# Transposed products of a decoder trunk: each tile's low matmul placed directly behind its high one

## Chip, core and metric

The kernel runs on one core of a Trainium2 chip. The metric is the device time of one execution in microseconds (us), as the median of several runs; beside it stands one execution taken by the hardware profiler, with a record of every instruction. TensorE is PE in the profile (PEld its weight loads), VectorE DVE, ScalarE ACT, GpSimd POOL, and SP the queue that issues most DMAs.

## What is computed

A decoder trunk of two layers on 256 tokens of width 2048 in float32: layer 0 mixes with a gated DeltaNet, layer 1 with sparse attention under an indexer; each layer goes on with a layer norm, a gated MLP of width 5120, another layer norm and a gated addition. Cut to its outline:

```python
for i in range(DEPTH):                                   # DEPTH = 2
    h = gdn_mixer(x, ...) if i % 2 == 0 else dsa_mixer(x, ...)
    x = layer_norm(DN_ALPHA * x + h, ln1_g[i], ln1_b[i])
    f = (silu(causal_dwconv(x @ ffn_w_gate[i], ffn_conv_w[i])) * (x @ ffn_w_up[i])) @ ffn_w_down[i]
    x = layer_norm(DN_ALPHA * x + f, ln2_g[i], ln2_b[i])
    x = x + sigmoid(x @ ple_w_gate[i]) * (p[i] @ ple_w_proj[i])
```

Nearly all of the work is products of x, or of what was made from it, with weight matrices that are read once.

## The kernel before

**High and low parts.** Each float32 operand of a weight product is held as two float32r numbers, a high part and what is left of it, the low part. A product is high x high + low x high + high x low. For x both parts lie in xT, [128, 16 row tiles, 2 parts, 256 tokens]. For a weight, `weights` (L86) loads a block of 512 KB into `raw` (4 buffers), ACT copies it to `hi` (L96), and DVE subtracts that from `raw` to give `lo` (L97). `hi` and `lo` have two buffers each: the `hi` of a block is written into the buffer of the block two earlier, as soon as PE has done its last matmul with it. `high_priority` lets the scheduler place both far ahead.

**Two kinds of products.** `gemm_steps` (L125) gives [tokens, columns]; the change leaves it alone. `gemm_t_steps` (L100) gives the transpose, [columns, tokens], and takes 256 columns of weights as two tiles of 128, each with a PSUM bank `q` of its own. One block is 4 row tiles of those 256 columns; 4 blocks make a sum. For each row tile and each column tile there are two matmuls: one with `hi` as the stationary operand, over both parts of x (512 columns, into the whole of q, L113), and one with `lo` over the high part of x alone (256 columns, into the second half of q, L117). So a block has 8 of the first and 8 of the second. Their order in a block is written out by the two loops at L111 and L115. There are 4176 of each in the program, in the DeltaNet's keys, queries and values, the indexer and the attention, and the MLP's gate and up projections.

**What follows a sum.** When the fourth block is done, the caller's `done` folds the halves of q: ACT copies the second half (L166), DVE adds it to the first (L167), and the caller goes on with ACT and DVE (for the MLP's gate a convolution, L621, L623, L625; for its up projection L630 and the split L170, L171).

**Order.** The scheduler of the framework sets one fixed order for each engine; each engine then works strictly in it and waits on semaphores. Between the matmuls of a block it also puts other PE work: in the DeltaNet small products and transposes, at the start of an MLP the layer norm's transposes (L250).

Of the kernel before, what the change touches and what calls it, by code (L numbers as in the profile page):

```python
# [18 lines left out]
D = 2048  # L19
# [10 lines left out]
# Columns of the table of constants.  # L30
# [4 lines left out]
def constants():  # L35
    """Masks, the identity and the buckets of relative distance: functions of the shapes alone."""
    c = np.zeros((P, N_CONST), np.float32)
    i, j = np.arange(P)[:, None], np.arange(P)[None, :]
    c[:, C_IDENT:C_IDENT + P] = i == j
    c[:, C_TRI:C_TRI + P] = i <= j  # L40
    c[:, C_OFF:C_OFF + P] = i // 32 > j // 32
    c[:, C_CMIN:C_CMIN + P] = np.where(j <= i, np.float32(3.4e38), np.float32(-BIG))
    x = np.zeros((4, 32, 8, 32), np.float32)
    for cg in range(4):
        for k in range(8):
            x[cg, :, k, 4 * k + cg] = 1.0
    c[:, C_XINIT:C_XINIT + 256] = x.reshape(P, 256)
    c[:, C_ONES:C_ONES + P] = 1.0
    c[:, C_CAUSAL:C_CAUSAL + P] = j <= i
    d = np.maximum(255 - np.arange(NR), 0)  # L50
    f = np.maximum(d, 1).astype(np.float32)
    large = 16 + (np.log(f / np.float32(16)) / np.float32(math.log(8.0)) * np.float32(16)).astype(np.int32)
    b = np.where(d < 16, d, np.minimum(large, 31))
    return c, (np.arange(32)[:, None] == b[None, :]).astype(np.float32)


def bcast(ap, n, axis):
    """ap with a new axis of n repeats."""
    dims = [list(x) for x in ap.ap]
    dims.insert(axis, [0, n])  # L60
    return bass.AP(tensor=ap.tensor, offset=ap.offset, ap=dims)


class Trunk:
# [21 lines left out]
    def weights(self, src, rows, nk, cols):  # L86
        """src: DRAM [K, N]; the block of nk row tiles from `rows` and `cols` as (hi, lo) [128, nk, ncols]."""
        nc = self.nc
        c0, n = cols
        shape = [P, nk, n]  # L90
        raw = self.wp.tile(shape, F32, tag="raw", name="raw", bufs=4)
        nc.sync.dma_start(out=raw, in_=src[rows:rows + nk * P, c0:c0 + n].rearrange("(k p) n -> p k n", p=P))
        hi = self.wp.tile(shape, F32R, tag="hi", name="hi", bufs=2)
        lo = self.wp.tile(shape, F32R, tag="lo", name="lo", bufs=2)
        with self.tc.high_priority(offset=W_AHEAD):
            nc.scalar.activation(hi, raw, AF.Copy)  # L96
            nc.vector.tensor_tensor(lo, raw, hi.bitcast(F32), op=ALU.subtract)  # L97
        return hi, lo

    def gemm_t_steps(self, src, c0, n, x, done, kt=KT):  # L100
        """Products with the output transposed, [columns, tokens], one call of done(column, psum) per 128
        columns; the sum of the two halves of psum is the product. Yields after each block of weights."""
        nc = self.nc
        for c in range(c0, c0 + n, 256):
            w = min(256, c0 + n - c)
            nt = [(o, min(P, w - o)) for o in range(0, w, P)]
            ps = [self.mm.tile([P, 512], F32, tag="mm", name="mm_ps") for _ in nt]
            nk = 1024 // w
            for k0 in range(0, kt, nk):
                hi, lo = self.weights(src, k0 * P, nk, (c, w))  # L110
                for k in range(nk):  # L111
                    for (o, m), q in zip(nt, ps):
                        nc.tensor.matmul(q[:m, :], hi[:, k, o:o + m], x[:, k0 + k].rearrange("p a b -> p (a b)"),  # L113
                                         start=k0 + k == 0, stop=False)
                for k in range(nk):  # L115
                    for (o, m), q in zip(nt, ps):
                        nc.tensor.matmul(q[:m, S:], lo[:, k, o:o + m], x[:, k0 + k, 0, :],  # L117
                                         start=False, stop=k0 + k == kt - 1)
                if k0 + nk < kt:
                    yield  # L120
            for (o, m), q in zip(nt, ps):
                done((c - c0 + o) // P, q[:m, :])
            yield

    def gemm_steps(self, src, c0, n, x, kt, done):  # L125
        """One block of at most 512 columns, [tokens, columns]: done(half, psum) for each half of the tokens."""
# [21 lines left out]
    @staticmethod  # L148
    def go_(*steps):
        """Runs the products of several calls side by side."""  # L150
        steps = list(steps)
        while steps:
            steps = [g for g in steps if next(g, steps) is not steps]
# [7 lines left out]
    def fold(self, pool, out, ps):  # L161
        """out = the product that gemm_t left in the two halves of ps."""
        nc = self.nc
        m = ps.shape[0]
        t = pool.tile([P, S], F32, tag="fold", name="fold", bufs=2)
        nc.scalar.activation(t[:m], ps[:, S:], AF.Copy)  # L166
        nc.vector.tensor_tensor(out, ps[:, :S], t[:m], op=ALU.add)  # L167
# [5 lines left out]
    def to_xT(self, xT, x, a, k0):  # L173
        """Four row tiles of xT for half a of the tokens from x [128, 512]."""
# [5 lines left out]
    def rows(self, pool, src, n, tag, bufs=1):  # L180
        """A DRAM row of n, in all partitions."""
# [4 lines left out]
    def columns(self, pool, srcs, tag):  # L186
        """DRAM arrays [n, 128], as columns of one tile [128, sum of n]."""
# [13 lines left out]
    def residual(self, xb, ps, st):  # L201
        """x <- ALPHA x + ps for a block of columns, and its moments."""
        self.nc.vector.scalar_tensor_tensor(xb, xb, ALPHA, ps, op0=ALU.mult, op1=ALU.add)
        self.nc.vector.bn_stats(st, xb)

    def moments(self, pool, st, eps):
        """Mean and 1/sqrt(variance + eps) from the statistics st [128, n, 6]."""
# [6 lines left out]
    def rsqrt(self, pool, z, n):  # L214
        """1 / sqrt(z) of z [128, n] > 0, which is overwritten: three Newton steps from a first value within 4%,
        by the exponent."""
# [13 lines left out]
    def layer_norm(self, pool, st, g, b, gb):  # L230
        """x and xT from the sums in x: g and b are rows in DRAM, gb the same as columns."""
# [35 lines left out]
    def gdn_gates(self, pool, w, gk):  # L267
# [7 lines left out]
        # softplus(x) = max(x, 0) + log1p(e), e = exp(-|x|); log1p(e) = 2 atanh(s), s = e / (2 + e) <= 1/3  # L275
# [16 lines left out]
        # beta = 1 / (1 + exp(-b))  # L292
# [4 lines left out]
        # running sums of g within each half of the tokens: as columns, and as rows by way of DRAM  # L297
# [13 lines left out]
    def gdn(self):  # L311
# [3 lines left out]
        with tc.tile_pool(name="gk", bufs=1) as gk, tc.tile_pool(name="gw", bufs=1) as pool:  # L315
            cw = gk.tile([P, 4, 64], F32, tag="cw", name="cw")
            ng = gk.tile([P, 1], F32, tag="ng", name="ng")
            # staged where the groups' tiles will be
# [24 lines left out]
    def gdn_groups(self, pool, gk, cw, ng, oT, load, gates):  # L343
        """Groups of two heads of queries and keys, four of values. In each half of the tokens, with k and q not
        normalised, c = beta / |k|^2: (I + L) u = beta v / |k|, L[t, s] = c_t (k_t . k_s) D[t, s] for s < t;
        o_t = (sum over s <= t of (q_t . k_s) D[t, s] u_s) / |q|. The blocks of 32 on the diagonal of I + L are
        inverted by substitution into T, then I + L = T^-1 (I + W), W = T (L outside the blocks), W^4 = 0."""
# [12 lines left out]
        def conv(n0, out):  # L360
            """gemm_t's consumer: causal convolution of the column tile, then 2 silu() into out(n)."""
# [13 lines left out]
        def decays(s):  # L375
            """D for s <= t, with s in the partitions (within a half: qd; from half to half: qo), and with t (L)."""
# [32 lines left out]
        def sums(s):  # L409
            """Sums of squares of q and k, as columns, and what follows from them."""  # L410
# [24 lines left out]
        def blocks(s):  # L435
# [15 lines left out]
            # the 32 by 32 blocks on the diagonal, one in each partition  # L451
# [12 lines left out]
            # their inverses by columns: column 4 c + e is number c in partition (e, block)  # L464
# [20 lines left out]
        def inverses(s):  # L485
            """T, transposed, and W, transposed."""
# [47 lines left out]
        def outputs(s):  # L534
            """o, normalised and gated, transposed."""
# [111 lines left out]
    def prepare(self, i, pool):  # L647
        """The taps of the MLP's convolution, as columns. The products p Wp: two blocks of columns with each call of
        what is returned, into self.pw."""
# [45 lines left out]
    def distances(self, pool):  # L695
        """The bias by distance in DRAM, F[h, 255 - distance], one copy per query. Yields between its transfers."""
# [19 lines left out]
    def dsa(self, pool, xT, oT):  # L716
# [3 lines left out]
        # indexer keys and head weights  # L720
# [17 lines left out]
        # scores of the indexer  # L738
# [18 lines left out]
        # each query's bias by distance, from its copy a place further on  # L757
# [12 lines left out]
        # the 64 largest of the causal scores: a mask of 0 or -1e30, added to the bias  # L770
# [12 lines left out]
        # keys, values  # L783
# [92 lines left out]
```

## Time and profile before

| | us |
|---|---|
| median of 3 runs | 2972.67 (2970.65 to 2974.01) |
| span of the profiled execution | 2969.3 |
| PE busy | 2859.2 (96%) |
| DVE busy | 1903.4 (64%) |
| ACT busy | 1398.3 (47%) |
| POOL busy | 486.1 (16%) |
| mean granted TensorE clock | 0.988 of full speed |

The median lies 3.4 us above the profiled span. PE's busy time is the union of its matmuls' records; since a matmul's record reaches over the start of the next, the time that one costs is read from start to start, not from its length. Times in the timeline are rounded to 0.01 us, so a cost per matmul is taken over a run of several.

### The profile page before, as it was taken

How to read it: one execution, taken by the hardware profiler on the slowest of the kernel's cores; microseconds unless marked ns; L12 is line 12 of the kernel's file. 1: busy time of each engine (PE TensorE's matmuls, PEld its weight loads, DVE VectorE, ACT ScalarE, POOL GpSimd, SP SyncE). 2: the span in 40 equal slices, each digit the busy share in tenths (PEclk: the TensorE clock that was granted, in tenths of full speed). 3: DMA queues.
4: the chain of work that ended last, by engine and by line, in shares of the span. 5: the costliest groups of instructions: out<-in, count | busy, mean ns of one | idle time of the engine just before them, and what ended most of it. 6: DMA issues, size and time to landing. Idle time of an engine off the chain costs nothing. (4 is left out here: it accounts for less than half of the span.)

```text
span 2969.3 us, 41861 instructions
## 1 busy us (share of the span) xinstructions
PE 2859.2 (96%) x15790; PEld 2450.0 (83%) x15790; DVE 1903.4 (64%) x3080; ACT 1398.3 (47%) x2143; POOL 486.1 (16%) x780
## 2 busy tenths in 40 slices
PE   8799999999899899999999899999989999999989
PEld 6688888888679788888888788888878888888877
DVE  6578777788444866666554755656586666655475
ACT  4345455455333545555433443455355555543344
POOL 1553344443200400000000300110040000000030
PEclk9899999999999999999999999999999999999999
DMA  6555555655465575666555456554656666655545
GB/s 194 147 146 146 155 161 162 168 149 143 141 195 190 173 224 187 191 186 191 186 189 186 151 181 198 171 159 140 202 171 188 188 191 186 191 186 188 186 153 181
DMA packets 425883, 520.94 MB, mean 175 GB/s; under 512 B 28204, under 2 KB 329648, under 8 KB 425424
## 3 DMA queue, kind: packets, MB, share of 16 engines
q1 hardware_dynamic: 418576, 499.91, 55.4%
q0 software_dynamic: 7104, 18.35, 2.2%
q8 instruction: 124, 2.03, 0.3%
q14 instruction: 79, 0.65, 0.1%
HBM read 513.94 MB, written 7.39 MB: 176 GB/s over the span
## 5 line engine op out<-in xcount | busy, mean ns | idle before, releaser
L97 DVE TENSOR_TENSOR lo<-raw,hi 128x1024 fp32r<-128x1024 f32 x925 | 1159.8, 1255 | 898.2 <-ACT hi L96 874.5
L96 ACT ACTIVATE hi<-raw 128x1024 fp32r<-128x1024 f32 x925 | 978.1, 1058 | 1320.1 <-PE b_ps L137 584.8
L113 PE MATMUL mm_ps<-xT,hi 128*128 128x512 f32 x4176 | 1077.7, 397 | 11.4 <-ACT hi L96 6.8
L113 PEld LDWEIGHTS mm_ps<-xT,hi 128*128 128x128 f32 x4176 | 752.0, 190 | 147.7 <-ACT hi L96 7.4
L117 PEld LDWEIGHTS mm_ps<-xT,lo 128*128 128x128 f32 x4176 | 573.5, 191 | 46.3 <-DVE lo L97 6.4
L117 PE MATMUL mm_ps<-xT,lo 128*128 128x256 f32 x4176 | 596.9, 285 | 4.7 <-DVE lo L97 4.7
L263 POOL TENSOR_TENSOR x<-x,lng 128x512 f32<-128x512 f32 x32 | 50.7, 1602 | 1535.5 <-PE n_ps L250 1529.1
L136 PE MATMUL b_ps<-hi,hT 128*128 128x512 f32 (+1 forms) x800 | 268.0, 350 | 0.0
L137 PE MATMUL b_ps<-hi,hT 128*128 128x512 f32 (+1 forms) x800 | 267.7, 350 | 0.0
L136 PE MATMUL b_ps<-hi,xT 128*128 128x512 f32 (+1 forms) x576 | 224.3, 393 | 6.2 <-ACT hi L96 5.7
L137 PE MATMUL b_ps<-hi,xT 128*128 128x512 f32 (+1 forms) x576 | 224.1, 392 | 0.6 <-DVE xT L258 0.6
L140 PE MATMUL b_ps<-lo,hT 128*128 128x512 f32 (+1 forms) x800 | 176.5, 350 | 0.0
L136 PEld LDWEIGHTS b_ps<-hi,hT 128*128 128x128 f32 x800 | 150.7, 188 | 22.0
L137 PEld LDWEIGHTS b_ps<-hi,hT 128*128 128x128 f32 x800 | 150.8, 188 | 21.9
L140 PE MATMUL b_ps<-lo,xT 128*128 128x512 f32 (+1 forms) x576 | 160.8, 395 | 4.1 <-DVE lo L97 4.1
L140 PEld LDWEIGHTS b_ps<-lo,hT 128*128 128x128 f32 x800 | 131.2, 188 | 22.0
L470 POOL TENSOR_TENSOR xt<-ld,xi 128x60 f32<-128x60 f32 (+24 forms) x248 | 124.7, 503 | 92.8 <-DMA ld<-lt 74.0
L136 PEld LDWEIGHTS b_ps<-hi,xT 128*128 128x128 f32 x576 | 110.0, 191 | 28.6 <-ACT hi L96 6.5
L137 PEld LDWEIGHTS b_ps<-hi,xT 128*128 128x128 f32 x576 | 110.2, 192 | 22.1 <-DVE xT L258 1.4
L140 PEld LDWEIGHTS b_ps<-lo,xT 128*128 128x128 f32 x576 | 106.8, 192 | 26.0 <-DVE lo L97 5.8
L136 PE MATMUL b_ps<-hi,oT 128*128 128x512 f32 (+1 forms) x320 | 107.9, 353 | 3.6 <-ACT hi L96 3.6
L137 PE MATMUL b_ps<-hi,oT 128*128 128x512 f32 (+1 forms) x320 | 108.0, 353 | 0.0
(258 smaller groups left out, 2712.0 us busy)
## 6 DMA issues: line engine op xcount, KB each, us to landing
raw<-in_gdn_w_in SPq DMA_DIRECT2D x193, 512.0 KB, 3.9
raw<-in_ffn_w_gate SPq DMA_DIRECT2D x160, 512.0 KB, 3.6
raw<-in_ffn_w_up SPq DMA_DIRECT2D x160, 512.0 KB, 3.6
raw<-in_ffn_w_down SPq DMA_DIRECT2D x160, 512.0 KB, 3.5
raw<-in_dsa_w_in SPq DMA_DIRECT2D x80, 512.0 KB, 3.6
raw<-in_gdn_w_o SPq DMA_DIRECT2D x64, 512.0 KB, 3.7
raw<-in_ple_w_gate SPq DMA_DIRECT2D x64, 512.0 KB, 3.7
raw<-in_dsa_w_o SPq DMA_DIRECT2D x32, 512.0 KB, 3.6
```

The lines of the kernel that those rows point to most:

```text
L96: nc.scalar.activation(hi, raw, AF.Copy)
L97: nc.vector.tensor_tensor(lo, raw, hi.bitcast(F32), op=ALU.subtract)
L113: nc.tensor.matmul(q[:m, :], hi[:, k, o:o + m], x[:, k0 + k].rearrange("p a b -> p (a b)"), start=k0 + k == 0, stop=False)
L117: nc.tensor.matmul(q[:m, S:], lo[:, k, o:o + m], x[:, k0 + k, 0, :], start=False, stop=k0 + k == kt - 1)
L136: nc.tensor.matmul(ps[a][:, :n], xh, hi[:, k, :], start=k0 + k == 0, stop=False)
L137: nc.tensor.matmul(ps[a][:, :n], xl, hi[:, k, :], start=False, stop=False)
L140: nc.tensor.matmul(ps[a][:, :n], x[:, k0 + k, 0, a * P:(a + 1) * P], lo[:, k, :], start=False, stop=k0 + k == kt - 1)
L263: nc.gpsimd.tensor_tensor(x[:, a, cs], x[:, a, cs], gr, op=ALU.mult)
L470: nc.gpsimd.tensor_tensor(tmp[:, :m, :w], bcast(ld[:, i + 1:, i], m, 1), xi[:, :m, i:i + 1].to_broadcast([P, m, w]), op=ALU.mult)
```

## The change

The two loops over a block's row tiles become one: the matmul with a tile's low part stands directly behind the one with its high part. The number of instructions, their shapes, their operands and the buffers are the same. Comments and docstrings are dropped too, which alters line numbers only (L117 of before is L115 of after, and later lines are two lower).

```diff
                 for k in range(nk):
                     for (o, m), q in zip(nt, ps):
                         nc.tensor.matmul(q[:m, :], hi[:, k, o:o + m], x[:, k0 + k].rearrange("p a b -> p (a b)"),
                                          start=k0 + k == 0, stop=False)
-                for k in range(nk):
-                    for (o, m), q in zip(nt, ps):
                         nc.tensor.matmul(q[:m, S:], lo[:, k, o:o + m], x[:, k0 + k, 0, :],
                                          start=False, stop=k0 + k == kt - 1)
```

The first place is PE in the first block of layer 0's MLP, where transposes of the layer norm (n_ps) stand between the matmuls. Before:

```order
L113 MATMUL mm_ps<-xT,hi 128x512 x3
L250 MATMUL n_ps<-ident,x 128x128
L113 MATMUL mm_ps<-xT,hi 128x512
L117 MATMUL mm_ps<-xT,lo 128x256 x3
L250 MATMUL n_ps<-ident,x 128x128 x6
L117 MATMUL mm_ps<-xT,lo 128x256 x5
L113 MATMUL mm_ps<-xT,hi 128x512 x8
L117 MATMUL mm_ps<-xT,lo 128x256 x8
```

And now, a part of the same block with buffer numbers (mm_ps_9445 and mm_ps_9446 are the sums of the two column tiles):

```order
L113 MATMUL mm_ps_9445<-xT_75,hi_9449 128x512
L248 MATMUL n_ps_9390<-ident_72,x_7839 128x128
L115 MATMUL mm_ps_9445<-xT_75,lo_9450 128x256
L113 MATMUL mm_ps_9446<-xT_75,hi_9449 128x512
L115 MATMUL mm_ps_9446<-xT_75,lo_9450 128x256
L248 MATMUL n_ps_9380<-ident_72,x_7839 128x128 x3
L248 MATMUL n_ps_9390<-ident_72,x_7839 128x128 x3
```

High and low matmuls of a block alternate, and a transpose can now stand between the two of a pair.

The second place is ACT in the middle of the same MLP, where a sum of the gate projection (mm_ps_13240 and mm_ps_13241) has just been finished and the blocks hi_13350, hi_13372, hi_13394 and hi_13416 of the up projection follow. Before:

```order
L96 ACTIVATE hi_13350<-raw_13348 128x1024
L96 ACTIVATE hi_13372<-raw_13370 128x1024
L166 ACTIVATE fold_13330<-mm_ps_13240 128x256
L166 ACTIVATE fold_13338<-mm_ps_13241 128x256
L621 ACTIVATE fac_13333<-fpd0_9441,fcw_8449 128x256
L96 ACTIVATE hi_13394<-raw_13392 128x1024
L621 ACTIVATE fac_13341<-fpd1_9442,fcw_8449 128x256
L625 ACTIVATE fac_13333<-fac_13333 128x256
```

And now:

```order
L96 ACTIVATE hi_13350<-raw_13348 128x1024
L164 ACTIVATE fold_13330<-mm_ps_13240 128x256
L96 ACTIVATE hi_13372<-raw_13370 128x1024
L619 ACTIVATE fac_13333<-fpd0_9441,fcw_8449 128x256
L164 ACTIVATE fold_13338<-mm_ps_13241 128x256
L96 ACTIVATE hi_13394<-raw_13392 128x1024
L623 ACTIVATE fac_13333<-fac_13333 128x256
L619 ACTIVATE fac_13341<-fpd1_9442,fcw_8449 128x256
```

The first of the two folds has moved ahead of the split of hi_13372, the second behind it; the rest of the gate's work is spread over the splits that follow.

## Rows read from the trace of the kernel before

**Rows 1.** The page's engine totals, and who PE waited for (total, times, longest).

```profile
PE 2859.2 (96%) x15790; PEld 2450.0 (83%) x15790; DVE 1903.4 (64%) x3080; ACT 1398.3 (47%) x2143; POOL 486.1 (16%) x780
...
PE mm_ps L113 <- ACT hi L96: 6.8, 3, 2.4
...
PE mm_ps L117 <- DVE lo L97: 4.7, 3, 3.3
```

**Rows 2.** The page's groups of instructions: busy, mean ns of one, idle before.

```profile
L113 PE MATMUL mm_ps<-xT,hi 128*128 128x512 f32 x4176 | 1077.7, 397 | 11.4 <-ACT hi L96 6.8
...
L117 PE MATMUL mm_ps<-xT,lo 128*128 128x256 f32 x4176 | 596.9, 285 | 4.7 <-DVE lo L97 4.7
```

**Rows 3.** Timeline of layer 0's MLP, PE and weight loads: start, length, instructions merged.

```profile
1201.63 2.00 PE L113 MATMUL mm_ps<-xT,hi 128*128 128x512 f32 x8
...
1203.47 1.12 PE L117 MATMUL mm_ps<-xT,lo 128*128 128x256 f32 x8
...
1204.31 1.70 PEld L113 LDWEIGHTS mm_ps<-xT,hi 128*128 128x128 f32 x8
1204.42 2.00 PE L113 MATMUL mm_ps<-xT,hi 128*128 128x512 f32 x8
...
1206.27 1.12 PE L117 MATMUL mm_ps<-xT,lo 128*128 128x256 f32 x8
...
1207.22 2.00 PE L113 MATMUL mm_ps<-xT,hi 128*128 128x512 f32 x8
```

**Rows 4.** Timeline of PE, narrow windows inside those runs: where their parts start.

```profile
1205.59 0.61 PE L113 MATMUL mm_ps<-xT,hi 128*128 128x512 f32 x2
...
1206.38 1.00 PE L117 MATMUL mm_ps<-xT,lo 128*128 128x256 f32 x7
```

**Rows 5.** Timeline of PE in the DeltaNet: transposed products behind 512-column matmuls of L140.

```profile
211.28 1.07 PE L140 MATMUL b_ps<-lo,xT 128*128 128x512 f32 x4
212.18 1.98 PE L113 MATMUL mm_ps<-xT,hi 128*128 128x512 f32 x8
214.00 1.11 PE L117 MATMUL mm_ps<-xT,lo 128*128 128x256 f32 x8
214.95 2.00 PE L113 MATMUL mm_ps<-xT,hi 128*128 128x512 f32 x8
216.79 1.12 PE L117 MATMUL mm_ps<-xT,lo 128*128 128x256 f32 x8
```

**Rows 6.** Timeline of ACT and DVE in the stretch of rows 3.

```profile
1203.67 1.06 ACT L96 ACTIVATE hi<-raw 128x1024 fp32r<-128x1024 f32 x1 [1.73 <-PE mm_ps L113]
...
1204.64 0.64 ACT L166 ACTIVATE fold<-mm_ps 128x256 f32<-128x256 f32 x2
1204.76 1.23 DVE L97 TENSOR_TENSOR lo<-raw,hi 128x1024 fp32r<-128x1024 f32 x1 [1.57 <-ACT hi L96]
1205.91 0.75 DVE L167 TENSOR_TENSOR fpd<-mm_ps,fold 128x256 f32<-128x256 f32 x2
...
1206.90 0.48 DVE L623 SCALAR_TENSOR_TENSOR fac<-fpd,fcw,fac 128x256 f32<-128x256 f32 x1 [0.24 <-ACT fac L621]
```

**Rows 7.** Timeline of the start of layer 1's MLP, PE and DVE.

```profile
2183.23 2.00 PE L113 MATMUL mm_ps<-xT,hi 128*128 128x512 f32 x8
2188.49 1.21 PE L117 MATMUL mm_ps<-xT,lo 128*128 128x256 f32 x8 [3.26 <-DVE lo L97]
2189.54 3.22 PE L113 MATMUL mm_ps<-xT,hi 128*128 128x512 f32 x8
...
2186.16 2.28 DVE L97 TENSOR_TENSOR lo<-raw,hi 128x1024 fp32r<-128x1024 f32 x1
```

**Rows 8.** Timeline of the start of layer 0's MLP, PE.

```profile
997.53 1.22 PE L117 MATMUL mm_ps<-xT,lo 128*128 128x256 f32 x8 [0.61 <-DVE lo L97]
998.59 2.00 PE L113 MATMUL mm_ps<-xT,hi 128*128 128x512 f32 x8
1001.47 1.21 PE L117 MATMUL mm_ps<-xT,lo 128*128 128x256 f32 x8 [0.88 <-DVE lo L97]
```

**Rows 9.** The DeltaNet: busy time by engine in 100 to 800 us, and a slow split.

```profile
100.00:800.00 700.00, 655.01 (x3807) 561.70 (x3806) 522.55 (x1170) 344.52 (x660) 299.88 (x589) 0.98 0.54 148
...
171.42 1.99 DVE L97 TENSOR_TENSOR lo<-raw,hi 128x1024 fp32r<-128x1024 f32 x1 [0.46 <-ACT hi L96]
```

## The prediction

> **What bounds the kernel now.** I read the totals first: PE is busy 96% of the span, and in all it waited 6.8 us for a hi and 4.7 us for a lo at the transposed products [rows 1]. So what counts is what PE's own matmuls cost from start to start, and whether the new order makes PE wait. The two groups that the change moves are 4176 matmuls of 512 columns ("high") and 4176 of 256 ("low") [rows 2]; their record lengths (397 and 285 ns) overlap, so I take the cost from the timeline. In the MLP a block starts at 1201.63, the next at 1204.42, the next at 1207.22: 2.795 us for 8 + 8 matmuls, 0.3494 us a pair; the eight high ones take 1.84 to 1.85, the eight low ones 0.95 [rows 3]. Nothing between them is idle: PE is the bound, and the total moves by whatever a pair moves, 4.2 us for each 0.001 us.
>
> **The change, part one: the pair on PE.** No instruction is added or removed. What changes is each matmul's neighbour: now 1 of 8 high ones follows a low one, and 1 of 8 low ones a high one; then all do. Inside the runs the cost is not uniform. Of the high run that starts at 1204.42 the first five take 1.17 (to 1205.59), 0.234 each, the last three 0.68 (to 1206.27), 0.227 each [rows 3, 4]. That this comes from the low ones ahead is shown by a high run that stands behind 512-column matmuls instead: 1.82 in all, 0.227 each, while the next, behind a low run, takes 1.84 [rows 5]. So short matmuls leave something behind that slows the next five long ones by about 0.007 each, and that wears off. Of the low run the first takes 0.11 (1206.27 to 1206.38), the other seven 0.84 together, 0.12 each [rows 3, 4]; 0.95 less 0.84 is again 0.11, with 0.01 of rounding, so I use 0.115.
>
> In the new order a high one never gets five long ones in a row to recover in. Its nearest row is therefore the early part of a run, 0.234; if one low matmul does too little to disturb it, it is 0.227. A low one directly behind a high one has 0.115 as its nearest row, but that one stood behind three undisturbed high ones; if the disturbance stays, it is 0.12 as for the rest. The bounds for a pair are 0.227 + 0.115 = 0.342 (0.0074 less than now, over 4176 pairs a gain of 31 us) and 0.234 + 0.12 = 0.354 (0.0046 more, a loss of 19 us). The literal neighbours give 0.234 + 0.115 = 0.349, nothing. Since the 0.115 was measured in a calmer state than the new order has, I take a value between that and the upper end, nearer to the lower, because both its parts have a row: 0.351, 0.0016 more than now, and 0.0016 x 4176 = **+7 us**.
>
> **Part two: the chain through ACT and DVE, in steady state.** The hi buffer becomes free with a block's last high matmul. Now that is the eighth of the run: it starts 0.23 ahead of the low run, at 1203.24, and the split into that buffer starts at 1203.67, 0.43 later; ACT takes 1.06, DVE starts 0.03 behind it and takes 1.23, to 1205.99 [rows 3, 6]. That lo belongs to the block that starts at 1207.22, whose low run comes 1.84 later, at 1209.06: 3.07 us to spare, which is why lo is hardly ever waited for. In the new order the last high one starts seven pairs into the block, 7 x 0.351 = 2.46. Then 2.46 + 0.43 + 1.06 + 0.03 + 1.23 = 5.21 us from the block's start to lo. The block two later starts at 2 x 8 x 0.351 = 5.62, and its very first low matmul needs lo; with 0.05 for the wake-up (DVE done at 2188.44, PE starts at 2188.49 [rows 7]) the slack is 0.36. So the cover falls from 3.07 to 0.36 us, but it holds. Where a sum ends, ACT now does one fold ahead of the split, as the order shows; it is 0.32 long [rows 6] and is released by a low matmul about one pair ahead of the last high one's end, so it delays the split by at most 0.2, and 0.16 is left. On DVE the gate's pieces between two splits are at most a fold addition (0.37) and two of L623 (0.5 each), 1.4 in all, against 2.81 - 1.23 = 1.58 free [rows 6]. The transfers have more: raw is released 0.85 later than now, out of four buffers of 2.8 us each. I cost the MLPs at nothing. In the DeltaNet DVE is busy 523 of 700 us, and a split there can take 1.99 instead of 1.23 [rows 9]; I found seven of that kind, one in each group but the last. Each exceeds the slack by 0.76 - 0.36 = 0.4: **+3 us**. If every group's end there and in the attention also slipped past the slack by 0.2, some 60 sums would add 12, the upper bound of this term; the lower is 0.
>
> **Part three: the starts of the MLPs.** There DVE still works on the layer norm, and lo comes late: PE does its eight high ones from 2183.23, then waits 3.26 us until 2188.49 [rows 7]. In the new order only one high matmul may go ahead; the other seven, 7 x 0.23 = 1.6 us, follow after the wait. In layer 0's MLP the same holds at 997.53 and 1001.47 [rows 8], where the second wait is the DVE's chain again, so that I count 1.6 once. With 1 us for the kernel's first products, **+4 us** (3 to 8: the high run behind that wait takes 3.22 instead of 2.00 us, so a longer wait could also keep PE slow for longer). Matmuls behind the waiting one can't pass it: PE stood idle for those 3.26 us with the next block's work queued [rows 7]. The Trainium skill says this as a rule ("TensorE: Matmul & The Clock Gate", Step-by-step: what each phase is for: only weight loads are pulled ahead, matmuls stay in program order), and the trace agrees.
>
> **The sum** against the profiled execution: 2969.3 + 7 + 3 + 4 = 2983.3 us; with the 3.4 us by which the median of the runs lies above that span, 2987.
>
> **The rivals.**
> *The pair gets faster.* If one low matmul between two high ones disturbs nothing, a pair costs 0.342: -31 us, and with 5 for waits and starts 2972.7 - 26 = 2947. For it: the high ones do come back to 0.227, and the first low one is quicker than the rest. Against: the recovery takes five long ones in the trace. Chance 0.25.
> *The order makes no difference on PE.* A low matmul hides the loading of the next weights, a high one too, and each pair has one of both in either order: the load goes out as the matmul ahead starts (1204.31 for the high run at 1204.42 [rows 3]). Then a pair stays at 0.3494, and only waits and starts remain, 2972.7 + 5 = 2978. Chance 0.25. The Trainium skill has a rule that gives this result (same page, LDWEIGHTS: the time of a load is the number of its columns over 1.2 GHz, 107 ns for 128): by it the low matmul's cost is set by the load beneath it, and the order can't matter; the 0.12 of the rows is near that figure, but the first one's 0.11 and the high ones' change from 0.234 to 0.227 don't follow from it.
> *The slack of 0.36 is not enough.* If in the steady blocks a split comes over 0.36 us late, PE stands at the first low matmul of a block. One such wait of 0.3 us in each of the 130 or so sums is 39 us: 2972.7 + 7 + 4 + 39 = 3023. It decides from a delay of 0.36 on; ACT and DVE have 1.6 us free in each block, which speaks against it. Chance 0.1.
> That the change doesn't do what it says is ruled out by the order, where the two kinds alternate.
>
> **How the numbers follow.** The forecast (a pair of about 0.351) gets 0.4, the rivals 0.25, 0.25 and 0.1. About 0.2% (6 us) is what a measurement of this kernel tells from no change. The faster rival is all below that; the unchanged pair's +5 lies within it, save a fifth; of the forecast's +14 I put some 0.33 above and 0.07 within. Faster 0.25, same 0.27, slower 0.48. The ends come from the bounds: -31 + 4 = -27 gives 2946, and +19 + 8 + 6 = +33 gives 3006, where I leave out the far side of the third rival. Forecast 2987, range 2946 to 3006; the forecast's own range is 2978 to 2996.
>
> **What would show it.** In the timeline of an MLP block, pairs from start to start: 0.351, with 0.342 and 0.349 as the rivals' values. The split L96 should start about 2.9 us after its block's start instead of 2.04, L97 should end less than half a microsecond ahead of the block that uses it, and PE's waits for lo in the MLPs' steady part should stay near zero. At an MLP's start the wait for lo should grow by about 1.5 us. I am wrong if PE's waits for lo grow by tens of microseconds, or if a pair falls below 0.347.

## The result, and the profile after

The changed kernel takes 2988.85 us (median of 4 runs, 2987.73 to 2989.74); the kernel before, beside it, 2972.23. The ratio is 1.0055, 95% interval 1.004 to 1.0069: slower by 16.6 us, where 2987 was forecast.

The page of the changed kernel: engine totals, who PE waited for, and the two groups that the change moves (busy, mean ns of one | idle before). They answer [rows 1, 2].

```profile
PE 2871.2 (96%) x15790; PEld 2448.5 (82%) x15790; DVE 1915.4 (64%) x3080; ACT 1402.6 (47%) x2143; POOL 493.0 (17%) x780
...
PE mm_ps L115 <- DVE lo L97: 9.6, 9, 2.7
...
PE mm_ps L113 <- ACT hi L96: 8.2, 4, 3.3
...
L113 PE MATMUL mm_ps<-xT,hi 128*128 128x512 f32 x4176 | 1497.3, 401 | 10.5 <-ACT hi L96 8.2
L115 PE MATMUL mm_ps<-xT,lo 128*128 128x256 f32 x4176 | 1187.0, 284 | 9.7 <-DVE lo L97 9.6
```

The busy times of the groups rose by hundreds of microseconds only because the records of the two kinds now overlap each other; the waits, where time could really be lost, rose by 4.9 and 1.4 us out of 17. Most of the rest is in the matmuls' spacing. In the timeline of PE in layer 0's MLP, where [rows 3] stood before, each matmul is now a row of its own (start, length):

```profile
1199.93 0.40 PE L113 MATMUL mm_ps<-xT,hi 128*128 128x512 f32 x1
1200.17 0.28 PE L115 MATMUL mm_ps<-xT,lo 128*128 128x256 f32 x1
1200.28 0.40 PE L113 MATMUL mm_ps<-xT,hi 128*128 128x512 f32 x1
1200.51 0.28 PE L115 MATMUL mm_ps<-xT,lo 128*128 128x256 f32 x1
1200.63 0.40 PE L113 MATMUL mm_ps<-xT,hi 128*128 128x512 f32 x1
1200.87 0.28 PE L115 MATMUL mm_ps<-xT,lo 128*128 128x256 f32 x1
1200.99 0.40 PE L113 MATMUL mm_ps<-xT,hi 128*128 128x512 f32 x1
```

Three pairs, 1199.93 to 1200.99, take 1.06 us: 0.3533 a pair, not 0.3494. In the records' nanoseconds the six starts are 241, 120, 236, 113, 233 and 117 apart, 1060 in all, and this comes back again and again.

A second view shows it over long stretches: how many high matmuls (L113 in every kernel here) two stretches inside the MLPs hold, as x in the third column. A matmul that reaches in from ahead is counted too, so a count is one or two high. Before:

```profile
1110.00:1420.00 310.00, 222.32 (x890) 1.00 0.61 189
2230.00:2600.00 370.00, 265.52 (x1061) 1.00 0.61 188
```

After:

```profile
1110.00:1420.00 310.00, 310.00 (x878) 1.00 0.61 186
2230.00:2600.00 370.00, 370.00 (x1049) 1.00 0.60 186
```

With one taken off, 370 us / 1060 is 0.349 and 370 / 1048 is 0.353. The granted clock is 1.00 in all of them, so it is not the clock.

Comparing the starts of the same matmul in the two traces gives the 17.1 us between the spans (2969.3 and 2986.4) by place: +3.3 ahead of layer 0's MLP, +1.5 at its start, +3.5 at one place near 1080 us, +10.5 from the pairs in the two MLPs (320 blocks at 0.033 more), -3 between the two MLPs; the rest is below 1.

### The profile page after: what moved, and what is told of

Read it like the earlier page. It is cut to its first block, busy times and chain, and to the rows that moved or that the text cites. A ratio compares the mean times of both kernels' runs of the same rounds, so it can differ in the third digit from the quotient of the medians.

```text
span 2986.4 us, 41886 instructions
## 1 busy us (share of the span) xinstructions
PE 2871.2 (96%) x15790; PEld 2448.5 (82%) x15790; DVE 1915.4 (64%) x3080; ACT 1402.6 (47%) x2143; POOL 493.0 (17%) x780
## 5 line engine op out<-in xcount | busy, mean ns | idle before, releaser
L96 ACT ACTIVATE hi<-raw 128x1024 fp32r<-128x1024 f32 x925 | 978.3, 1058 | 1150.2 <-PE b_ps L135 582.6
L113 PE MATMUL mm_ps<-xT,hi 128*128 128x512 f32 x4176 | 1497.3, 401 | 10.5 <-ACT hi L96 8.2
L115 PE MATMUL mm_ps<-xT,lo 128*128 128x256 f32 x4176 | 1187.0, 284 | 9.7 <-DVE lo L97 9.6
L113 PEld LDWEIGHTS mm_ps<-xT,hi 128*128 128x128 f32 x4176 | 788.5, 189 | 200.0 <-ACT hi L96 9.4
L115 PEld LDWEIGHTS mm_ps<-xT,lo 128*128 128x128 f32 x4176 | 792.4, 190 | 15.4 <-DVE lo L97 13.9
L164 ACT ACTIVATE fold<-mm_ps 128x256 f32<-128x256 f32 x261 | 98.6, 378 | 189.1 <-PE mm_ps L115 189.1
L468 POOL TENSOR_TENSOR xt<-ld,xi 128x60 f32<-128x60 f32 (+24 forms) x248 | 113.9, 459 | 85.4 <-DMA ld<-lt 66.6
L470 POOL TENSOR_TENSOR xi<-xi,xt 128x60 f32<-128x60 f32 (+24 forms) x248 | 116.9, 471 | 19.4
```

The costliest lines, as they stand in the source:

```text
L468: nc.gpsimd.tensor_tensor(tmp[:, :m, :w], bcast(ld[:, i + 1:, i], m, 1), xi[:, :m, i:i + 1].to_broadcast([P, m, w]), op=ALU.mult)
L470: nc.gpsimd.tensor_tensor(xi[:, :m, i + 1:], xi[:, :m, i + 1:], tmp[:, :m, :w], op=ALU.subtract)
```

## The experiments

**Where the loss lies.** Two kernels share the change out, by an argument that chooses the order:

```diff
-    def gemm_t_steps(self, src, c0, n, x, done, kt=KT):
+    def gemm_t_steps(self, src, c0, n, x, done, kt=KT, alt=False):
...
+                if alt:
+                    for t in tiles:
+                        high(*t)
+                        low(*t)
+                else:
+                    for t in tiles:
+                        high(*t)
+                    for t in tiles:
+                        low(*t)
```

`mlp_only` sets it for the gate and up products, `all_but_mlp` everywhere else.

> Alternating order (high, low, high, low) in the gate and up products of the two MLPs alone, all other transposed products as in the kernel before. In the trace of the changed kernel the MLPs' pairs go from 0.3494 to 0.3533 us, the DeltaNet's and the attention's stay at about 0.350 to 0.352. If the whole loss lies in the MLPs: 2560 pairs x 0.0041 = +10.5, +1.7 at the starts, +3.5 at the one place in layer 0's MLP where a split waits for raw: +16, about 2988 us, as long as the changed kernel. If the loss were spread evenly over the 4176 pairs, the MLPs would hold 61% of it: about +10, 2982.

> The other half: alternating order everywhere but in the MLPs. Loss in the MLPs alone: within 2 us of the kernel before (DeltaNet +2 to +3.6, indexer +1.5, attention -3): 2972 to 2975. Loss spread evenly over the pairs: +6, 2979.

Measured: 2987.41 us (ratio 1.0051, 1.0034 to 1.0067) and 2971.89 (1.0002, 0.9992 to 1.0011), beside 2972.11. The loss lies in the MLPs. But the runs of `mlp_only` spread from 2980.23 to 2993.26, and its counts differ from those of the changed kernel in layer 0's MLP alone:

```profile
1110.00:1420.00 310.00, 310.00 (x896) 1.00 0.62 190
2230.00:2600.00 370.00, 370.00 (x1048) 1.00 0.60 186
```

896 where the changed kernel has 878 and the kernel before 890: 310 / 895 is 0.346, less than before. The starts in the records give 0.3533 in that MLP up to PE's wait at 1078 us, and 0.3467 from there to its end. (That this execution is still 12 us longer than the one before lies mostly, by the starts, in 3.4 at the first MLP's start, 4.1 at that wait and 5 in layer 1's pairs, less 2.5 from the pairs of 0.3467.) The same order of the same instructions has two steady costs, one above the 0.3494 of before and one below.

**What sets the cost of a pair.** `other_bank` lets a low matmul follow the high one of the next tile, whose sum is in another PSUM bank; `fours` does four of a kind at a time; `all_long` alternates, with 512 columns for the low ones too.

```diff
+                for i, t in enumerate(tiles):        # other_bank
+                    high(*t)
+                    if i:
+                        low(*tiles[i - 1])
+                low(*tiles[-1])
...
-                    nc.tensor.matmul(q[:m, S:], lo[:, k, o:o + m], x[:, k0 + k, 0, :],     # all_long
+                    nc.tensor.matmul(q[:m, :], lo[:, k, o:o + m], x[:, k0 + k].rearrange("p a b -> p (a b)"),
```

> Alternating in kind, but a low matmul follows the high one of the next tile, so that it never adds to the PSUM tile that the matmul ahead of it adds to (h0 h1 l0 h2 l1 ... h7 l6 l7). Theory A (a matmul costs by the lengths of the few ahead of it): a pair in the MLPs stays at about 0.353, 2987 to 2990 us in all. Theory B (a low matmul directly behind its own high one pays for adding to the same PSUM tile): the pair falls back to 0.349 or less, 2975 to 2980.

> Four high, four low, four high, four low in each block. Theory A (a high matmul needs some five long ones in a row to come back from 0.234 to 0.227 us): none of the high ones recovers, 4 x 0.2325 + 0.113 + 3 x 0.12 = 1.403 for four pairs, 0.3508 a pair, +5 to +7: about 2979. Theory C (each change from one length to the other costs a fixed time): the changed kernel's 16 changes a block cost 8 x 0.0039 = 0.031 us more than before's 2, so 4 changes cost 0.0045 us a block more than before, 0.3500 a pair: +2.3, about 2975.

> Alternating order, but the low part too is multiplied with both parts of x, 512 columns instead of 256 (one more, smaller term of the product is computed). Now the weights alternate as in the changed kernel and the lengths don't. Theory A and D (what costs is the change of length): every matmul at the calm 0.2267, 0.4533 a pair, 0.1007 x 4176 more than the changed kernel's: about 3410. Theory F (what costs is the alternation of hi and lo weights, or the adding into the same tile): 0.2267 + 2 x 0.0033, 0.460 a pair, about 3435.

Measured: 2986.79 (1.0053, 1.0036 to 1.007), 2982.06 (1.0035, 1.0024 to 1.0047) and 3394.37 us in one execution. The count of `other_bank` in layer 1's MLP:

```profile
2230.00:2600.00 370.00, 360.26 (x1050) 1.00 0.60 187
```

That is 0.3527; from the starts a pair is 0.3525 in both MLPs, so theory B falls: adding to the tile of the matmul ahead is not what costs. `fours` has 0.3500 in layer 0's MLP behind the wait near 1080 us, theory C's number, and 0.3508 ahead of it and in layer 1's, theory A's; both theories fall as they stood, since neither lets one order have two costs. Its total is 7 us more than its pairs explain: by the starts, +5.3 arose ahead of the first MLP, in the DeltaNet, and 4 at the stall near 1080 us, less 3 in the attention. Of `all_long`, a stretch of layer 0's MLP:

```profile
1200.00:1400.00 200.00, 171.63 (x442) 1.00 0.47 145
```

200 / 441 is 0.4535, twice 0.2267: where the lengths are equal, alternating hi and lo costs nothing, and theory F falls. (The whole lies 16 us below the expected 3410; by the starts 10 of them arose ahead of the first MLP, where PE's wait for a transfer, pm, fell from 26.6 to 7.7 us.) With 120 ns for a low matmul in the middle of a run and 226.7 for a high one in the calm part of a run [rows 4, 5], a pair without any disturbance would be 0.3467, the lower of the two costs. Only the sum agrees, though: in that rhythm (`mlp_only`, 1200 to 1420 us) a high one takes 231.7 ns and a low one 115.0 in the mean. That the lower cost is the undisturbed one is not shown.

**Two rhythms of one order.** `mlp_only_again` is a second trace of the same kernel. `kicks` is the changed kernel with one transpose of a 128x128 tile, read by nobody, after three of every four rounds of gate and up products:

```diff
+                if n // 2 % 4:
+                    y = (self.tri, hT[:, n, 0, 0:P].bitcast(F32),
+                         hT[:, n + 1, 0, 0:P].bitcast(F32))[n // 2 % 4 - 1]
+                    kick = self.sp.tile([P, P], F32, tag="sp", name="kick")
+                    nc.tensor.transpose(kick, y, self.ident)
```

> The same kernel as in the run with alternating order in the MLPs alone, one more execution with a trace. Its five times spread over 13 us, those of the changed kernel over 2. Theory D (a rhythm drawn at each wait): the MLPs' stretches need not have the same rhythm as in the first trace; 0.3467 or 0.3533, or each in another place. If the code alone fixed the rhythm: again 0.3533 until the stall near 1080 us, 0.3467 behind it, 0.3533 in layer 1's MLP.

> The changed kernel, and in each MLP, after three of every four rounds of gate and up products, PE transposes one 128x128 tile that nobody reads: a constant that is long there, the first column tile of hT just being made, or the second. The latter two make PE wait some 2 to 3 us for ACT and DVE. In the run with alternating order in the MLPs alone, layer 0's MLP went from 0.3533 us a pair to 0.3467 at PE's 3 us stall near 1080 us and stayed there to its end, while the changed kernel kept 0.3533 across the same stall. Theory D (the order has several steady rhythms, and each wait of PE draws one of them anew): the stretches between the transposes show both 0.3467 and 0.3533, constant within a stretch, changing only where PE waited. Theory E (0.3533 is what this order costs; the 0.3467 has another cause, in that kernel alone): all stretches at 0.3533. The waits themselves add 10 x 2.6 us in each MLP: about 3040 us in all, which is not what is being asked.

The second trace shows what the first did, 0.3533, then 0.3467 behind the wait, then 0.3533: in these two executions of one program the rhythm is the same, though not the time (2980.55 us here). In `kicks`, E falls and D holds in part: of 28 stretches between transposes 16 have 0.3533 and 11 have 0.3467, each constant within itself, and one changes from 0.3467 to 0.3533 at PE's wait near 1083 us. But the change isn't bound to a wait: eight of the ten transposes of a constant, for which PE doesn't wait, left 0.3467 behind them, each time in place of 0.3533. (The transposes of hT made PE wait 0.3 us each, not 2 to 3; hence 2994.69 us in all.)

`after_kicked` keeps three of the constant ones in each MLP (`if n // 2 in (1, 4, 7)`).

> The changed kernel with three transposes of a constant tile that nobody reads in each MLP (after the second, the fifth and the eighth of its 20 rounds of gate and up products); PE doesn't wait for them, each costs it about 0.1 us. In the run with many such transposes, one that found the rhythm of 0.3533 us with the last low matmul at 120 ns left 0.3467 behind it, seven times of seven. Theory D (two steady rhythms of one order, and any disturbance of PE may change from one to the other): most of layer 1's MLP and of layer 0's behind its stall at 0.3467, 0.0066 x some 1000 pairs each, 13 us less than the changed kernel: about 2976, and no slower than 2984 if only one MLP changes. If a wait were needed to change the rhythm: 0.3533 throughout, 2989.

Measured: 2978.71 us, ratio 1.0019 (1.0009 to 1.0028): 5.4 us slower than the kernel before beside it, where the changed kernel is 16.6 slower. The difference is made by six instructions that add work. The timeline of PE around the third one in layer 0's MLP, high matmuls of the same length on both sides:

```profile
1180.08 0.40 PE L113 MATMUL mm_ps<-xT,hi 128*128 128x512 f32 x1
...
1180.44 0.40 PE L113 MATMUL mm_ps<-xT,hi 128*128 128x512 f32 x1
...
1180.79 0.40 PE L113 MATMUL mm_ps<-xT,hi 128*128 128x512 f32 x1
...
1181.14 0.40 PE L113 MATMUL mm_ps<-xT,hi 128*128 128x512 f32 x1
...
1181.50 0.27 PE L650 MATMUL kick<-ident,cst 128*128 128x128 f32 x1
...
1181.96 0.40 PE L113 MATMUL mm_ps<-xT,hi 128*128 128x512 f32 x1
...
1182.31 0.39 PE L113 MATMUL mm_ps<-xT,hi 128*128 128x512 f32 x1
...
1182.65 0.40 PE L113 MATMUL mm_ps<-xT,hi 128*128 128x512 f32 x1
...
1183.00 0.39 PE L113 MATMUL mm_ps<-xT,hi 128*128 128x512 f32 x1
...
1183.34 0.40 PE L113 MATMUL mm_ps<-xT,hi 128*128 128x512 f32 x1
```

Ahead of it three pairs take 1.06 (1180.08 to 1181.14), behind it four take 1.38 (1181.96 to 1183.34), and so it stays. The counts of L113 in stretches ahead of the change and behind it, and of one behind that in layer 1's MLP (where the second transpose, at 2300.9, makes it):

```profile
1110.00:1170.00 60.00, 60.00 (x171) 1.00 0.59 186
1200.00:1420.00 220.00, 220.00 (x636) 1.00 0.61 190
2320.00:2600.00 280.00, 280.00 (x809) 1.00 0.60 190
```

60 / 170 is 0.353; 220 / 635 and 280 / 808 are 0.3465. A later transpose in layer 1 left 0.3467 as it was, and the other three left 0.3533. The one at 1113.5 us did so behind a low matmul of 120 ns, so the rule in the expectation (met with a low matmul at 120 ns, 0.3533 gives way to 0.3467; eight times of eight in `kicks`, not seven) doesn't hold.

**The place near 1080 us.** There layer 0's MLP has four transfers of 766 KB that copy a table (`fx`) in DRAM. They are issued on POOL's queue, the MLP's weights on SP's (not in the same queues, as the expectations below have it); both use the core's 16 DMA engines, whose mean busy share is 0.99 from 1076 to 1082 us after the change. Before, ACT and PE:

```profile
1077.50 1.06 ACT L96 ACTIVATE hi<-raw 128x1024 fp32r<-128x1024 f32 x1 [5.69 <-DMA raw<-in_ffn_w_up]
...
1078.61 2.14 PE L113 MATMUL mm_ps<-xT,hi 128*128 128x512 f32 x8 [2.36 <-ACT hi L96]
```

After:

```profile
1081.68 1.06 ACT L96 ACTIVATE hi<-raw 128x1024 fp32r<-128x1024 f32 x1 [6.16 <-DMA raw<-in_ffn_w_up]
...
1082.79 0.49 PE L113 MATMUL mm_ps<-xT,hi 128*128 128x512 f32 x1 [3.30 <-ACT hi L96]
1084.05 0.39 PE L115 MATMUL mm_ps<-xT,lo 128*128 128x256 f32 x1 [0.77 <-DVE lo L97]
...
1085.25 0.63 PE L113 MATMUL mm_ps<-xT,hi 128*128 128x512 f32 x1
...
1085.89 0.63 PE L113 MATMUL mm_ps<-xT,hi 128*128 128x512 f32 x1
```

A block comes 5.7 to 6.2 us late. In the old order PE still has its eight low matmuls to do in that time, and behind the wait eight high ones to cover the making of lo; in the new one it waits longer for hi, then again for lo, 4.07 us for 2.36. Behind that the granted clock is 0.50 from 1084.6 to 1087.9 us (1.2 GHz, the lower of its two levels): high matmuls stand 640 ns apart, five pairs take 3.19 us instead of 1.77. Behind the wait of before the clock stays at 1.00. So of the 3.5 us about half is waiting and about half the clock. Two kernels were to take the cause away:

```diff
+                    tick = pool.tile([P, 1], F32, tag="tick", name="tick")     # after_fx_spread
+                    nc.gpsimd.tensor_copy(tick, hT[:, n - 2, 0, 0:1].bitcast(F32))
...
+            hT = yield                                                         # after_fx_apart
+            if hT is not None:
+                nc.gpsimd.dma_start(out=fx[0:1, o:o + 1], in_=hT[0:1, 0:1].bitcast(F32))
             nc.gpsimd.dma_start(out=fx[:, o:o + R // 4],
```

> The changed kernel with the four large DRAM transfers of the bias by distance (fx) in layer 0's MLP held apart: each waits for the column tile of hT made just ahead of it, so that they no longer run one right after the other near 1070 us while the load of w_up is in the same queues. If they are why a split there waits 6 us for its raw block and PE stands 4 us: that wait goes, -3.5 us against the changed kernel, 2985, and with no wait there the rhythm of the pairs stays what it was at the MLP's start. If another transfer is what delays the load: no change, 2989.

> The changed kernel, each of the four fx transfers now made to wait for a column tile of hT that is made 45 us behind the last (by a transfer of four bytes from it into the place that the large one writes), since in the earlier run with spread transfers they still ran together at 1065 to 1085 us. If the four together are what keeps the load of w_up away: the split's wait of 6 us for raw is gone or below 1 us, PE's wait of 3.3 us there with it: -3.5 against the changed kernel, and if the rhythm of 0.3533 then holds, 2985. If PE's stall there stays at 3 us, something else delays the load.

The first didn't do what it says: the scheduler put the small copies elsewhere on POOL, and the four transfers still ran together. So its 2982.65 us (1.0042, 1.0027 to 1.0057) say nothing on them; what it gained is the rhythm, 0.3467 behind the stall. In the second the transfers start at 1087.2, 1133.1, 1178.3 and 1222.6 us, the trace names no wait of PE from 1060 to 1130 us, and by the starts 6.1 us are gone there, the whole stall and not only what the change had added. That the four together near 1070 us delayed the load is shown. Its median is 2981.38 us (1.0025, 1.0016 to 1.0033); its twelve runs reach from 2971.59 to 2984.52. The traced one is the shortest and has 0.3533 in layer 0's MLP from 1062 us on and 0.3467 in layer 1's (x1068 in 2230 to 2600 us). One MLP in the other rhythm is 1280 x 0.0066 = 8.5 us, about that spread, but of runs without a trace the rhythm isn't known.

**Two versions from what was learnt.** `mirrored` halves the changes of length: every second block does its low matmuls first.

```diff
+                if (k0 // nk) % 2:
+                    for t in tiles:
+                        low(*t, stop=False)
+                    for k, j in tiles:
+                        high(k, j, stop=k0 + k == kt - 1)
```

> From the kernel before: every second block does its eight low matmuls first and then its eight high ones, so that the runs are of 16 across the blocks' borders and the lengths change half as often. A block of before takes 2.7936 us, 16 calm matmuls would take 8 x 0.3467 = 2.7733: the two changes of length cost 0.020. Half of that is 0.010 x 522 blocks: -5 us, 2967. If the runs of 16 have a rhythm of their own without the disturbance, up to -10, 2962. If the lo of a mirrored block comes late (it is needed 1.84 us earlier there), each wait adds: over 2972.

Measured: 2981.88 us (1.0032, 1.002 to 1.0044). PE and its weight loads in layer 0's MLP:

```profile
1207.06 3.82 PE L113 MATMUL mm_ps<-xT,hi 128*128 128x512 f32 x16
1210.71 2.08 PE L118 MATMUL mm_ps<-xT,lo 128*128 128x256 f32 x16
1212.63 3.82 PE L113 MATMUL mm_ps<-xT,hi 128*128 128x512 f32 x16
1216.28 2.29 PE L118 MATMUL mm_ps<-xT,lo 128*128 128x256 f32 x16
...
1217.35 1.00 PEld L118 LDWEIGHTS mm_ps<-xT,lo 128*128 128x128 f32 x8 [0.16 <-DVE lo L97]
1218.40 0.85 PE L113 MATMUL mm_ps<-xT,hi 128*128 128x512 f32 x3
```

Two blocks take 5.57 (1207.06 to 1212.63), 0.02 less than two of before, as expected. But once in eight blocks the lo that is now needed 1.84 earlier comes late: the low run from 1216.28 takes 2.12 instead of 1.92, and more is lost than won, by the starts 4.5 us in the two MLPs. That was the expectation's last case. Another 3.4 is the stall near 1080 us.

`calm_mlps` alternates in the MLPs, but for their first pair of products, and in the attention's query products (L818), keeps separate runs elsewhere, holds the fx transfers apart and has the three constant transposes.

> What the runs so far point to, put together: alternating order in the MLPs (all but the first pair of gate and up products, where the lo is late) and in the attention's query products, separate runs everywhere else, the fx transfers apart as before, and the three constant transposes in each MLP. Theory D: the MLPs' pairs at 0.3467 for nearly all of their length, 2496 x 0.0025 = -6 against the kernel before; -2.4 for PE's wait near 1078 us, -3 in the attention, +0.6 for the transposes: -11, 2962, outside what a measurement can take for no change. If the transposes leave the MLPs at 0.3533: +10 - 2.4 - 3 + 0.6 = +5, 2978. One MLP in each rhythm: about 2970.

Measured: 2964.56 us (2959.53 to 2968.63), ratio 0.9972 (0.9963 to 0.9981) beside 2973.25: 8.7 us faster than the kernel before and outside the measurement's doubt. Its counts:

```profile
1110.00:1150.00 40.00, 40.00 (x114) 1.00 0.67 206
1200.00:1420.00 220.00, 220.00 (x636) 1.00 0.63 194
2400.00:2600.00 200.00, 200.00 (x578) 1.00 0.62 190
```

0.3467 for most of both MLPs, but 0.3533 from 1081 to 1171 us and from 2295 to 2354, where the third transpose changed it back. What had changed 0.3467 into 0.3533 is neither a transpose (the second ones stand at 1103.3 and 2286.7 us) nor a wait: each time one high matmul, the first of a block, takes 226 or 228 ns to the next start instead of 231, and from there the other cycle runs. So a start 3 to 5 ns early can be enough. Which way a disturbance goes wasn't found out.

The rhythm is the smaller part of this gain. In the traced execution, 5.3 us shorter than that of the kernel before, the starts give 2.7 us gained at the stall near 1080 us, 2.5 in the attention and some 1.8 in the MLPs' pairs, where 6 was expected; 1.6 is lost ahead of the first MLP.

## Why the prediction was right, and where its steps were not

**The pair.** The term that decided the sign was right in kind (a high matmul close behind a low one doesn't recover) and mis-sized: 0.0016 us a pair over all 4176, +7, against 0.0041 in the MLPs by the starts, +10.5, and no net loss elsewhere (`all_but_mlp`). The step that failed is the price of a high matmul in the new order. The forecast took 0.234, from the first five of a run, as the most that it would be (in the records' nanoseconds that row is 0.2324; the rest is rounding). In the MLPs' steady parts it is 0.2366 in the mean (233, 241 and 236 ns in turn), where before it is 0.2301; the low one is 0.1167, between the forecast's 0.115 and 0.12, where before it is 0.1191. That a pair still lies below the upper bound of 0.354 is luck: a high one above its bound and a low one under. Choosing one value, 0.351, failed as well: the order has no one value. PE goes round in a fixed cycle, and here it was the one of 0.3533 in both MLPs. The faster rival was real too, at 0.3467 instead of 0.342, and a change of the order elsewhere in the program can bring it about. So the sign that the prediction named against itself, a pair below 0.347, didn't come in the changed kernel's steady parts, but did for the same order in `mlp_only`. The rival that the order makes no difference fell. The Trainium skill's rule from which that rival followed ("TensorE: Matmul & The Clock Gate", LDWEIGHTS) gives a load one time, whatever stands ahead of it; the two rhythms, with the same loads in the same order, aren't explained by it. Nor is a load's record 107 ns long, the estimate by that rule: on the pages of the profile it is 190 ns in the mean for the high matmuls before, and 189 after.

**The chain through ACT and DVE.** Right step by step in the MLPs' steady parts. ACT and DVE after, where a block starts at 1201.34 and the one that needs this lo at 1206.99:

```profile
1204.01 0.38 ACT L164 ACTIVATE fold<-mm_ps 128x256 f32<-128x256 f32 x1 [1.47 <-PE mm_ps L115]
1204.29 1.05 ACT L96 ACTIVATE hi<-raw 128x1024 fp32r<-128x1024 f32 x1
...
1205.37 1.23 DVE L97 TENSOR_TENSOR lo<-raw,hi 128x1024 fp32r<-128x1024 f32 x1
```

The split starts 2.95 after its block (2.9 was forecast), behind one fold, and lo is there at 1206.60, 0.39 ahead of the block (0.36). PE waits for no lo in the MLPs' steady parts, so the third rival fell; `mirrored` shows what it looks like where the slack is gone.

**The DeltaNet.** Its +3 came (3.3 by 979 us; two traces of `mlp_only`, one kernel, differ by 1.8 there), but by luck, not from the seven slow splits: from 60 to 985 us PE waited for no lo at the transposed products. Between 50 and 72 us the changed kernel falls from 2 us ahead of the old one to 1 behind, and there PE's longest wait is now

```profile
PE ss_ps L416 <- ACT sq L413: 2.6, 1, 2.6
```

for a square that ACT makes (sums of squares of q and k); the longest wait there before was 1.1. The seven traces with high and low strictly alternating in the DeltaNet have this wait, 2.1 to 2.7 us long (`other_bank` 1.1); `before`, both traces of `mlp_only` and `calm_mlps`, with separate runs there, don't. That it is the reason was read from the traces, with ACT's order changed around it, and not tested by itself.

**The starts of the MLPs.** +4 was forecast; it was 1.5 in layer 0. In layer 1 the one wait for lo [rows 7] has become several:

```profile
2192.59 0.39 PE L115 MATMUL mm_ps<-xT,lo 128*128 128x256 f32 x1 [0.88 <-DVE lo L97]
...
2198.39 0.39 PE L115 MATMUL mm_ps<-xT,lo 128*128 128x256 f32 x1 [2.75 <-DVE lo L97]
...
2202.32 0.38 PE L115 MATMUL mm_ps<-xT,lo 128*128 128x256 f32 x1 [0.84 <-DVE lo L97]
```

4.47 in all for 3.26, +1.2 where 1.5 was forecast; but by the starts only 0.3 is lost there. What the forecast counted on top, slow matmuls behind a longer wait, didn't come here. Before, the run of 3.22 us [rows 7] is a stretch with the granted clock at 0.50, from 2190.0 to 2193.4 us, behind the wait. In the changed kernel the slow stretch lies ahead of the waits, 0.56 from 2180.9 to 2184.1 us, and behind them, from 2191 to 2200, the clock is 1.00.

**What the sum left out.** The stall near 1080 us, +3.5 above the pairs: its row [2.36 <-ACT hi L96] was there before, within the 6.8 us of [rows 1], and the rule of the starts (a wait that a run of eight used to cover) holds for it as well. It is here that the slow matmuls behind a longer wait came, about half of the 3.5. And the -3 between the MLPs, most of it in the attention, whose cause wasn't followed. The total came out within 2 us by luck, because a pair term too small by 3.5 and a missing 3.5 stood against starts too large by 2 and a gain of 3.

## What to carry to other kernels

Where PE is the bound and long and short matmuls mix, take their cost from start to start over hundreds of them, in each stage apart, and don't expect an order to have one price: look for stretches with different ones in the same trace before a gain or loss of half a per cent is put down to the order. One trace shows one draw of the rhythm; an instruction added elsewhere can change it. And an order that uses a second operand earlier spends the work that covered that operand's making, everywhere a load comes late and not only at the starts.

## What was not expected of the hardware

The same alternating order, at a granted clock of 1.00, runs for hundreds of microseconds at 0.3533 us a pair (starts 113, 233, 117, 241, 120 and 236 ns apart, three pairs) or at 0.3467 (mostly 231, 113, 232 and 118, two pairs), and one 128x128 transpose changes the one into the other, or (twice in `calm_mlps`) nothing but a start 3 to 5 ns early. A third cycle, 230 and 117, one pair, also 0.3467, stands in the changed kernel for a few us at the MLPs' starts, in `after_kicked` from 2369 to 2633 us and in `after_fx_apart` from 2206 to 2626. What in PE makes them stays open.

Runs of 512-column matmuls alone have two costs as well. The counts of all PE matmuls before, in layer 1's down projection and in the gated addition at the end:

```profile
2640.00:2680.00 40.00, 40.00 (x172) 1.00 0.56 185
2894.00:2914.00 20.00, 20.00 (x90) 1.00 0.63 210
```

0.2343 us each (by the starts) in the first, 0.2267 in the second, from the same lines of code. In the output and down projections it is 0.2343 in the traces before and after the change alike; whether it is a rhythm too or lies in the operands wasn't tried.
